# Sparse attention with the softmax weights as the stationary matmul operand, values with a ones column moving, and masks added by bf16 products

## Chip, cores and metric

One core of a Trainium2 chip. The metric is device microseconds of one execution. The kernel before takes 2502.95 us (median of 3 runs, 2499.74 to 2503.1).

## What is computed

One layer of a decoder trunk: 1024 tokens, width 1024. The part that changes is the sparse attention (NSA): 16 heads in 4 groups of 4, head size 64, three branches per head.

```python
s_c = einsum(q, kc) - slopes * dist_c                       # 63 compressed keys
p_c = softmax(where(dist_c >= 0, s_c, NEG)) * any_valid     # also chooses the key blocks
o_cmp = einsum(p_c, vc)
o_slc = selection_branch(q, rmsnorm(k_s), v_s, top_k blocks)  # softmax over chosen 64-token blocks
o_win = window_branch(q, rmsnorm(k_w), v_w)                 # softmax over the last 256 tokens
o = gates[..., 0:1] * o_cmp + gates[..., 1:2] * o_slc + gates[..., 2:3] * o_win
```

Around it stand the input projections with a gated DeltaNet (before), and the output projections and the MLP (after).

## The kernel before

The program is one recorded list: each step is a Python function that is put at a time and a rank by `at` (L312), and all are called in that order (L1373). Each engine gets its instructions in an order fixed at build time and runs them in that order.

**Stages.** Projections and DeltaNet come first, then the sparse attention, then output projection and MLP. The sparse attention has 32 items (L1358): group g of 4, query tile t of 8 (128 queries, 4 heads each). An item (L1105) has these steps, put by `at3` (L1098) at times around its number i, so that steps of several items interleave, together with the DeltaNet output projection (`dn_part`, tiles `g`):

- `cmp_scores` (L1131) to `cmp_out` (L1199): the compressed branch. A product with three rows of position terms (`far`, `onesr`, L1134) and two with the keys make scores in a PSUM tile `m` of a ring of two. VectorE adds the mask and takes the minimum head by head (L1142), ScalarE takes the exponential, VectorE multiplies by gate and inverse sum (L1171), TensorE transposes (L1184) and multiplies by the values (L1196); the result `acc` stands as channels by queries.
- `peak` (L1204): scores of each head against all keys (tiles `S`), whose minimum VectorE takes (L1217).
- `weights` (L1236), once for each key tile of 128 and branch (0 selection, 1 window), 228 times in all: two products into a PSUM tile `T` (128 keys by 4 heads x 128 queries), at the edge of the mask two more with a triangular `cap` (L1246: bf16, 64x64 blocks, tiles `cb`; 88 key tiles have them), then ScalarE writes the exponentials `P`. GpSimd adds the `P` tiles of a branch into `sum` (L1253, L1256).
- `values` (L1260): for each key tile two products, one for each pair of heads, with the values `vv` as the stationary operand (128 keys x 64 channels) and half of `P` moving (256 columns). The results go to two 64-row halves of PSUM tile `O`, which has a region of its own for each branch.
- `total` (L1266), `share` (L1271), `join` (L1281), once for each branch: two products with a matrix of ones sum `sum` over keys, VectorE transposes, inverts, multiplies by a gate (`gq`) and transposes back, then multiplies `O` by it, GpSimd adds to `acc`, and after branch 1 a DMA stores it to `ond`.

`gq` is a copy of the gates in a transposed layout, made once in `gating` (L407 to L417) by four products and 16 copies. `sparse_setup` (L1026) loads the constants.

All operands of `values`, `total` and of the products with the compressed keys and values are plain f32; TensorE runs such a product as two instructions. Each of these has a weight load (LDWEIGHTS) of its own.

Of the kernel before, what the change touches and what calls it, by code (L numbers as in the profile page):

```python
# [35 lines left out]
         ("msel", "mwin", "mcmp", "okm", "addm", "hot", "capd", "capw", "edge"))  # L36
# [6 lines left out]
def constants():  # L43
# [20 lines left out]
    c64 = np.arange(64)[None, :]  # L64
    capd = np.where(p % 64 <= c64, 0, 1e30).astype(f)
    capw = np.where(p % 64 > c64, 0, 1e30).astype(f)
# [26 lines left out]
    for br in range(2):  # L93
        for hl in range(2):
# [5 lines left out]
                 mwin=mwin, mcmp=mcmp, hot=hot, capd=capd, capw=capw, edge=edge, anyv=anyv, okm=okm, addm=addm)  # L100
# [48 lines left out]
def body(ctx: ExitStack, tc: tile.TileContext, A, out):  # L149
# [50 lines left out]
    def load_consts(pool, i):  # L200
        n = f"cst{i}"
        w = A[n].shape[1]
        cst[i] = pool.tile([128, (w + 63) // 64 * 64 if i == 2 else w], F32, name=n, bufs=1)[:, 0:w]
        SY.dma_start(cst[i], A[n])
# [182 lines left out]
    gq = PL.cq.tile([128, 2, NT, NG, 8], F32, name="gq")  # L387
# [8 lines left out]
    def gating():  # L396
# [9 lines left out]

        for qb in range(4):  # L407
            sl = pb.tile([128, 4, 32], F32, name="sl", bufs=2)
            V.tensor_copy(sl, ident[:, 32 * qb:32 * qb + 32].unsqueeze(1).to_broadcast([128, 4, 32]))
            pg = PL.ps.tile([128, NT, 4, 4, 3], F32, name="s")  # L410
            mm(pg.rearrange("p t g r c -> p (t g r c)"), sl.rearrange("p a b -> p (a b)"),
               gates.rearrange("p t c -> p (t c)"), True, True)
            for hf in range(2):
                for br in range(2):
                    o = slice(64 * hf, 64 * hf + 64)
                    V.tensor_copy(gq[o, br, :, :, qb::4].rearrange("p t g a -> p (t g) a"),
                                  pg[o, :, :, 2 * hf:2 * hf + 2, br + 1].rearrange("p t g a -> p (t g) a"))  # L417
# [605 lines left out]

    msel = mwin = mcmp = okm = addm = hot = ones = identb = capd = capw = onesr = far = QC = nsp = mts = O = None

    def sparse_setup():  # L1026
        nonlocal msel, mwin, mcmp, okm, addm, hot, ones, identb, capd, capw, onesr, far, QC, nsp, mts, O
# [3 lines left out]
        mcmp = K("mcmp").rearrange("p (t c) -> p t c", t=8)  # L1031
# [3 lines left out]
        ones = K("ones")  # L1035

        onesr = pn.tile([128, 128], F32R, name="onesr")
        identb, capd, capw = [pn.tile([128, w], BF16, name=f"cb{i}") for i, w in enumerate((128, 64, 64))]
        for o, n in ((identb, "ident"), (capd, "capd"), (capw, "capw"), (onesr, "ones")):
            V.tensor_copy(o, K(n))  # L1040
# [42 lines left out]
    def values_of(g):  # L1083
        for br in range(2):
            SY.dma_start(kk[g][2][:, :, br, :],
                         nvd[br, :, 64 * g:64 * g + 64].rearrange("(t p) c -> p t c", p=128))
# [16 lines left out]
    kk = {}  # L1103

    def item(i, g, t):  # L1105
# [25 lines left out]
        def cmp_scores():  # L1131
            psc = PL.pm.tile([128, 4, 64], F32, name="m")
            o = slice(32 * g, 32 * g + 3)
            mm(g2(psc), onesr[o], far[o], True, False)  # L1134
# [4 lines left out]
            sm = PL.pn.tile([128, 4], F32, name="csm", bufs=2)  # L1139
            for r in range(4):  # L1140
                o = 2 * (r % 2) + r // 2
                V.tensor_tensor_reduce(pc[:, o, :], psc[:, r, :], mcmp[:, t, :], 1.0, 3e38,  # L1142
                                       OP.add, OP.min, mx[:, o:o + 1])
            for r in range(4):
                act(pc[:, r, :], pc[:, r, :], AF.Exp, scale=-1.0, bias=mx[:, r:r + 1], accum_out=sm[:, r:r + 1])
            X["pc"], X["sm"] = pc, sm

        def cmp_choose():
            pc, sm = X["pc"], X["sm"]
            rc = PL.pn.tile([128, 4], F32, name="rc", bufs=2)  # L1150
# [20 lines left out]
            V.tensor_tensor(pc, pc, rc.unsqueeze(2).to_broadcast([128, 4, 64]), OP.mult)  # L1171

        def choice():
            X["ch"] = p = PL.pm.tile([80, 128], F32, name="m")
# [6 lines left out]
        def cmp_turn():  # L1181
            p = PL.pm.tile([128, 2, 128], F32, name="m")
# [9 lines left out]
        def cmp_values():  # L1192
            pT = X["pT"]
            p = PL.pm.tile([128, 256], F32, name="m")
            for b in range(2):
                mm(p[:, b * 128:(b + 1) * 128], vcb[:, g, :], pT[:, b, :], True, True)  # L1196
            X["acc"] = p

        def cmp_out():  # L1199
            p = X["acc"]  # L1200
            X["acc"] = acc = PL.pn.tile([128, 256], F32, name="acc", bufs=4)
            act(acc, p)
# [24 lines left out]
        def peak_rows():  # L1227
            X["pk"] = p = PL.pm.tile([112, 128], F32, name="m")
# [7 lines left out]
        def weights(br, k):  # L1236
# [7 lines left out]
            if cap is not None:  # L1244
                for q in Q2:
                    mm(ps[q, :, q], identb[q, q], cap[q].unsqueeze(1).to_broadcast([64, 4, 64]), False, True)  # L1246
            P = PL.pr.tile([128, 4, 128], F32, name="P", bufs=5)
            act(P, ps, AF.Exp, scale=-1.0)
            X[br, k] = P
            if spans[br][1] == 1:  # L1250
                X["sum", br] = P
            elif ("sum", br) in X:
                adds.tensor_tensor(X["sum", br], X["sum", br], P, OP.add)  # L1253
            elif ("one", br) in X:
                X["sum", br] = s = PL.pr.tile([128, 4, 128], F32, name=f"sum{br}", bufs=2 - br)
                adds.tensor_tensor(s, X.pop(("one", br)), P, OP.add)  # L1256
            else:
                X["one", br] = P

        def values(br, k, first, last):  # L1260
            vv = kk[g][2]
            P = X.pop((br, k))
            for hf in range(2):
                mm(O[hf * 64:hf * 64 + 64, br], vv[:, k, br, :], g2(P[:, 2 * hf:2 * hf + 2, :]), first, last)

        def total(br):  # L1266
            X["tot", br] = p = PL.pm.tile([128, 2, 128], F32, name="m")
            for hf in range(2):
                mm(p[hf * 64:hf * 64 + 64], ones[:, 0:64], g2(X["sum", br][:, 2 * hf:2 * hf + 2, :]), True, True)

        def share(br):  # L1271

            b = PL.pr.tile([128, 256], F32, name="bs", bufs=3)
            V.transpose(b, g2(X["tot", br]))
            c = PL.pr.tile([128, 16], F32, name="coef", bufs=4)[:, 0:8]
            V.reciprocal(c, b[:, 0::32])
            V.tensor_tensor(c, c, gq[:, br, t, g], OP.mult)
            X["bs", br] = b = PL.pr.tile([128, 256], F32, name="bs", bufs=3)
            V.transpose(b, c.unsqueeze(2).to_broadcast([128, 8, 32]))

        def join(br):  # L1281
            b = X["bs", br]
            V.tensor_tensor(b, O[:, br], b, OP.mult)  # L1283
            acc = X["acc"]
            GP.tensor_tensor(acc, acc, b, OP.add)
            if br == 1:
                SY.dma_start(ond[2 * g:2 * g + 2, :, t * 128:(t + 1) * 128].rearrange("a p q -> p a q"),
                             acc.rearrange("p (a q) -> p a q", a=2))
# [464 lines left out]
```

## Time and profile before

| what | value |
|---|---|
| median of 3 runs | 2502.95 us |
| the profiled execution | 2501.7 us, span 2499.9 us |
| TensorE (PE) busy | 2423.2 us, 97% of the span, 14193 matmul instructions |
| VectorE (DVE) / ScalarE (ACT) / GpSimd (POOL) busy | 1680.0 / 1099.2 / 768.4 us |
| sparse stage, about 1104 to 1668 us | PE, DVE, ACT, POOL work together |

A busy PE is not a PE at its peak: the modelled end of a matmul lies after the start of the next. So for PE the distance from one start to the next is read, which is what an instruction costs the queue. "Idle before" is time in which an engine did nothing, and the name behind the arrow is what ended it.

### The profile page before, as it was taken

The numbers are of one execution on the slowest core, as the hardware profiler recorded it, in microseconds if no ns is written. First come the engines' busy times: TensorE is split into PE (matmuls) and PEld (weight loads), VectorE is DVE, ScalarE is ACT, GpSimd is POOL, SyncE is SP. The second block draws the span as 40 slices with busy tenths as digits, with TensorE's granted clock in tenths as the row PEclk, the third lists the DMA queues.
The fourth block names the chain that finished last, engine by engine and source line by source line (L and its number), as shares of the span: only waits on it lengthen the run. The fifth ranks groups of instructions, "written<-read, shape, count | busy, mean of one in ns | idle before, by whom it ended". The sixth has DMA issues, their size and how long they took to land. (4 is left out here: it accounts for less than half of the span.)

```text
span 2499.9 us, 40066 instructions
## 1 busy us (share of the span) xinstructions
PE 2423.2 (97%) x14193; PEld 1865.5 (75%) x14193; DVE 1680.0 (67%) x4006; ACT 1099.2 (44%) x2258; POOL 768.4 (31%) x622
## 2 busy tenths in 40 slices
PE   8999999999999999999999999999998999989999
PEld 5787878788887888765555555558877888868887
DVE  7666574837576665368788797964368666586685
ACT  4233343434443442346565655442236555534443
POOL 3132220303132321003534445432135443360230
PEclk9999999999999999999999999999999999999999
DMA  5421313122221312264232322126433444477343
GB/s 174 126 76 45 86 44 88 48 79 63 62 66 57 82 48 82 73 174 129 87 85 73 110 60 72 47 80 217 162 124 131 144 156 144 149 256 231 120 125 102
DMA packets 237353, 267.17 MB, mean 107 GB/s; under 512 B 76961, under 2 KB 128481, under 8 KB 237025
## 3 DMA queue, kind: packets, MB, share of 16 engines
q1 hardware_dynamic: 237152, 264.61, 34.3%
q8 instruction: 112, 1.84, 0.3%
q14 instruction: 89, 0.72, 0.1%
HBM read 190.12 MB, written 72.38 MB: 105 GB/s over the span
## 5 line engine op out<-in xcount | busy, mean ns | idle before, releaser
L179 PE MATMUL g<-hh,wh 128*128 128x512 f32 (+1 forms) x816 | 336.0, 412 | 6.5 <-ACT hh L176 6.1
L179 PE MATMUL g<-hl,wh 128*128 128x512 f32 (+1 forms) x816 | 328.7, 403 | 0.1
L179 PE MATMUL g<-hh,wl 128*128 128x512 f32 (+1 forms) x816 | 323.9, 397 | 0.0
L179 PE MATMUL V<-big,wh 128*128 128x512 f32 x768 | 239.0, 392 | 2.4 <-DVE c L1596 2.4
L188 DVE TENSOR_TENSOR wl<-a,wh 128x512 fp32r<-128x512 f32 x192 | 160.3, 836 | 112.2 <-ACT wh L176 111.9
L176 ACT ACTIVATE wh<-wr 128x512 fp32r<-128x512 f32 x210 | 132.0, 629 | 216.1 <-PE g L179 137.7
L176 ACT ACTIVATE wh<-a 128x512 fp32r<-128x512 f32 x192 | 121.0, 630 | 222.0 <-PE V L179 112.3
L1217 DVE CUSTOM_DVE_ANT_0 junk<-S,cst 128x384 f32<-128x384 f32 (+3 forms) x320 | 167.7, 528 | 63.1 <-PE S L179 61.9
L279 DVE TENSOR_TENSOR wl<-wr,wh 128x512 fp32r<-128x512 f32 x178 | 127.5, 720 | 113.4 <-ACT wh L176 110.2
L176 ACT ACTIVATE P<-T 128x512 f32<-128x512 f32 x228 | 134.2, 594 | 144.8 <-PE T L179 124.7
L179 PEld LDWEIGHTS g<-hh,wh 128*128 128x128 f32 (+1 forms) x816 | 153.8, 188 | 35.2 <-ACT hh L176 6.1
L179 PEld LDWEIGHTS g<-hh,wl 128*128 128x128 f32 (+1 forms) x816 | 153.6, 188 | 29.7 <-issue 0.6
L179 PEld LDWEIGHTS g<-hl,wh 128*128 128x128 f32 (+1 forms) x816 | 154.0, 189 | 26.6 <-DVE hl L326 1.3
L179 PEld LDWEIGHTS V<-big,wh 128*128 128x128 f32 x768 | 144.6, 189 | 33.5 <-ACT c L176 2.0
L1253 POOL TENSOR_TENSOR sum<-sum,P 128x512 f32<-128x512 f32 x101 | 133.7, 1324 | 70.1 <-ACT P L176 67.7
L179 PE MATMUL V<-big,wl 128*128 128x512 f32 x384 | 150.3, 391 | 3.2 <-DVE wl L188 3.2
L179 PE MATMUL g<-wh,hh 128*128 128x256 f32 x512 | 147.5, 288 | 0.0
L179 PE MATMUL o<-P,vv 128*64 128x256 f32 x912 | 144.2, 399 | 1.8 <-DVE bs L1283 1.6
L179 PE MATMUL g<-wl,hh 128*128 128x256 f32 x512 | 144.8, 283 | 0.0
L179 PE MATMUL g<-wh,hl 128*128 128x256 f32 x512 | 144.8, 283 | 0.0
L179 PE MATMUL S<-ks,qc 96*128 96x384 f32 (+3 forms) x320 | 122.9, 397 | 6.8 <-DVE mx L1217 6.3
L1453 POOL TENSOR_TENSOR a<-a,a 128x512 f32<-128x512 f32 x32 | 51.1, 1596 | 254.5 <-DVE wl L188 228.5
(378 smaller groups left out, 6010.0 us busy)
## 6 DMA issues: line engine op xcount, KB each, us to landing
bb<-acd SPq DMA_DIRECT2D x112, 256.0 KB, 2.8
wr<-in_w_dn_dram SPq DMA_DIRECT2D x64, 256.0 KB, 2.7
a<-in_w_u_dram SPq DMA_DIRECT2D x64, 256.0 KB, 3.3
acd<-c SPq DMA_DIRECT2D x64, 256.0 KB, 2.3
a<-in_w_d_dram SPq DMA_DIRECT2D x64, 256.0 KB, 5.0
wr<-in_w_nb_dram SPq DMA_DIRECT2D x32, 256.0 KB, 2.6
wr<-in_w_gt_dram SPq DMA_DIRECT2D x32, 256.0 KB, 2.6
gtd<-fx SPq DMA_DIRECT2D x32, 256.0 KB, 2.1
```

The source lines that it names most:

```text
L176: return SC.activation(o, i, fn, **kw)
L179: return PE.matmul(o, l, r, start=start, stop=stop, skip_group_check=True)
L188: V.tensor_tensor(lo, src, f(hi), OP.subtract)
L279: V.tensor_tensor(wl, wr, f(wh), OP.subtract)
L1217: V.tensor_tensor_reduce(junk[:, :w], ps[:, :w], mask[:, a:b], 1.0, 3e38, OP.add, OP.min, o)
L1253: adds.tensor_tensor(X["sum", br], X["sum", br], P, OP.add)
L1453: (eng or GP).tensor_tensor(o, a, b, OP.subtract)
```

## The change

`values` swaps its operands: `P` (64 queries of one head) is stationary, and the values move, with a column of ones as 65th; eight products for a key tile. `O` then stands as queries by channels, and its column 64 is the softmax sum. So `total`, `share`, the `sum` additions and `gq` go. `O` is now one region for both branches. The values of two key tiles follow each other. `join` divides by column 64; after branch 1 `turn_out` transposes `acc` back on TensorE and `turn_store` copies and stores it. The triangular caps become one bf16 product of 512 columns; the mask of the compressed scores is added by a bf16 product too, and the position terms use all 128 rows with a selecting column `gsel`. VectorE takes the four minima of the compressed scores in one reduction, and multiplies by gate and inverse sum where the branch's result is read (`cmp_out`).

```diff
-        for qb in range(4):
...
-            mm(pg.rearrange("p t g r c -> p (t g r c)"), sl.rearrange("p a b -> p (a b)"),
-               gates.rearrange("p t c -> p (t c)"), True, True)
...
+        for o, sign, base in ((capd, 1, 0), (capw, -1, -1)):
+            GP.memset(o, 0.0)
+            GP.affine_select(o, o, [[sign, 128]], OP.is_ge, 1e30, base=base, channel_multiplier=-sign)
+        maskb = pn.tile([128, 8, 64], BF16, name="maskb")
...
-        O = PL.po.tile([128, 2, 256], F32, name="o")
+        O = PL.po.tile([128, 4, 128], F32, name="o")
...
-        vv = p.tile([128, NT, 2, 64], F32, name="vv")
+        vv = p.tile([128, NT, 2, 128], F32, name="vv")
+        GP.memset(vv[:, :, :, 64:65], 1.0)
...
-            mm(g2(psc), onesr[o], far[o], True, False)
+            mm(g2(psc), gsel[:, g:g + 1].to_broadcast([128, 128]), far, True, False)
+            mm(psc, identb, maskb[:, t:t + 1, :].to_broadcast([128, 4, 64]), False, False)
...
+            V.tensor_reduce(mx, psc, axis=AX.X, op=OP.min)
             for r in range(4):
                 o = 2 * (r % 2) + r // 2
-                V.tensor_tensor_reduce(pc[:, o, :], psc[:, r, :], mcmp[:, t, :], 1.0, 3e38,
-                                       OP.add, OP.min, mx[:, o:o + 1])
-            for r in range(4):
-                act(pc[:, r, :], pc[:, r, :], AF.Exp, scale=-1.0, bias=mx[:, r:r + 1], accum_out=sm[:, r:r + 1])
+                act(pc[:, o, :], psc[:, r, :], AF.Exp, scale=-1.0, bias=mx[:, r:r + 1], accum_out=sm[:, o:o + 1])
...
-            V.tensor_tensor(pc, pc, rc.unsqueeze(2).to_broadcast([128, 4, 64]), OP.mult)
+            X["rc"] = rc
...
-                mm(p[:, b * 128:(b + 1) * 128], vcb[:, g, :], pT[:, b, :], True, True)
+                mm(p[:, b * 128:(b + 1) * 128], pT[:, b, :], vcb[:, g, :], True, True)
...
-            act(acc, p)
+            V.tensor_tensor(acc, p, X["rc"].unsqueeze(2).to_broadcast([128, 4, 64]), OP.mult)
...
-                for q in Q2:
-                    mm(ps[q, :, q], identb[q, q], cap[q].unsqueeze(1).to_broadcast([64, 4, 64]), False, True)
-            P = PL.pr.tile([128, 4, 128], F32, name="P", bufs=5)
+                mm(ps, identb, cap.unsqueeze(1).to_broadcast([128, 4, 128]), False, True)
+            P = PL.pr.tile([128, 4, 128], F32, name="P", bufs=6)
...
-            if spans[br][1] == 1:
-                X["sum", br] = P
-            elif ("sum", br) in X:
-                adds.tensor_tensor(X["sum", br], X["sum", br], P, OP.add)
...
-            for hf in range(2):
-                mm(O[hf * 64:hf * 64 + 64, br], vv[:, k, br, :], g2(P[:, 2 * hf:2 * hf + 2, :]), first, last)
-        def total(br):
...
-        def share(br):
...
+            for r in range(4):
+                for q in Q2:
+                    mm(O[q, 2 * (r % 2) + r // 2, 0:65], P[:, r, q], vv[:, k, br, 0:65], first and r == 0, last)
         def join(br):
-            b = X["bs", br]
-            V.tensor_tensor(b, O[:, br], b, OP.mult)
+            c = PL.pr.tile([128, 64], F32, name="coef", bufs=2)[:, 0:4]
+            V.reciprocal(c, O[:, :, 64])
+            V.tensor_tensor(c.rearrange("p (b a) -> p b a", b=2), c.rearrange("p (b a) -> p b a", b=2),
+                            gt.rearrange("p (a b) c -> p b a c", a=2)[:, :, :, br + 1], OP.mult)
+            b = PL.pr.tile([128, 4, 64], F32, name="bs", bufs=2)
+            V.tensor_tensor(b, O[:, :, 0:64], c.unsqueeze(2).to_broadcast([128, 4, 64]), OP.mult)
             acc = X["acc"]
-            GP.tensor_tensor(acc, acc, b, OP.add)
...
+            adds.tensor_tensor(acc, acc, b, OP.add)
+        def turn_out():
+            X["out"] = p = mtile(128, 2, 128)
+            for b in range(2):
+                PE.transpose(p[:, b, :], g2(X["acc"][:, 2 * b:2 * b + 2, :]), ident)
+        def turn_store():
+            o = PL.pr.tile([128, 2, 128], F32, name="ot", bufs=2)
+            act(o, X["out"])
+            SY.dma_start(ond[2 * g:2 * g + 2, :, t * 128:(t + 1) * 128].rearrange("a p q -> p a q"), o)
...
+            j0 = j - (0 if br == 0 else t + 1)
+            e = i + (j + (j0 % 2 == 0 and not last)) / n + lag
+            times.append(e)
+            at3(e, values, br, k, first, last)
```

The order of the instructions moves with it. TensorE around the end of the window branch (branch 1) of group 1, query tile 6, before. `o` is `O`, `cst_114` with `sum` the matrix of ones, `T`/`S`/`m` are the PSUM tiles named above; a program row with x2 is two products:

```order
L179 MATMUL o<-P,vv 64x256 x2
L179 MATMUL S<-ks,qc_11341 128x128
L179 MATMUL T<-qd,kd 128x512
L179 MATMUL T<-qc_11348,ks 128x512
L179 MATMUL m<-sum_14752,cst_114 64x256 x2
L179 MATMUL o<-P,vv 64x256 x2
L179 MATMUL m<-far,onesr 128x256
L179 MATMUL m<-kcb,qn 128x128 x2
L179 MATMUL T<-qd,kd 128x512
L179 MATMUL T<-qc_11348,ks 128x512
L179 MATMUL S<-ks,qc_11341 128x128
L179 MATMUL o<-P,vv 64x256 x2
```

The first row is the branch's last key tile; the next item's first key tile follows five rows below and its second at the end. The same place after the change:

```order
L177 MATMUL o<-vv,P 64x65 x8
L177 MATMUL S<-ks,qc_11318 128x128
L177 MATMUL T<-qd,kd 128x512
L177 MATMUL T<-qc_11325,ks 128x512
L177 MATMUL m<-far,gsel 128x256
L177 LDWEIGHTS cb_11296
L177 MATMUL m<-maskb,cb_11296 128x256
L177 MATMUL m<-kcb,qn 128x128 x2
L177 MATMUL T<-qd,kd 128x512
L177 MATMUL T<-qc_11325,ks 128x512
L177 MATMUL S<-ks,qc_11318 128x128
L177 MATMUL o<-vv,P 64x65 x16
```

The total has gone, the next item's first two key tiles are one run of 16 products at the end, and a mask product stands behind `far`.

VectorE at the same place before (`share`, then the compressed scores of a later item; ISA rows of L1142 are its minima):

```order
L1274 STREAM_TRANSPOSE bs<-m 128x256
L1276 RECIPROCAL coef<-bs 128x8
L1277 TENSOR_TENSOR coef<-coef,gq 128x8
L1279 STREAM_TRANSPOSE bs<-coef 128x256
L1142 ISA pc,cmx<-m,cst_11327 128x64
```

`join` (L1283) follows behind the other minima. After the change (`join` in the rows of `coef` and `bs`; rows of L1223 are `peak`'s minima, `cmx` is the reduction of the compressed scores):

```order
L1208 TENSOR_TENSOR acc<-m,rc 128x256
L1266 RECIPROCAL coef<-o 128x4
L1223 ISA junk,mx<-S,cst_11294 128x128
L1267 TENSOR_TENSOR coef<-coef,gates 128x4
L1270 TENSOR_TENSOR bs<-o,coef 128x256
L1148 TENSOR_REDUCE cmx<-m 128x4
```

Between the first and the last reading of `O` (L1266, L1270) stands work of another item.

## Rows read from the trace of the kernel before

**Rows 1.** The page's busy time of TensorE (busy us, share of the span, instructions) and its granted clock in 40 slices, and the sparse stage without its start, from the view of stretches (length, then busy us of each engine with its instructions, granted clock, DMA share, GB/s).

```profile
PE 2423.2 (97%) x14193; PEld 1865.5 (75%) x14193; DVE 1680.0 (67%) x4006; ACT 1099.2 (44%) x2258; POOL 768.4 (31%) x622
PEclk9999999999999999999999999999999999999999
...
1121.00:1668.00 547.00, 532.99 (x2790) 304.50 (x2790) 449.12 (x1613) 304.51 (x754) 250.22 (x218) 1.00 0.27 79
```

**Rows 2.** The timeline of TensorE at several places in the sparse stage: start us, length us, engine, line, operation, tiles, shape, instructions merged in the row, idle time before with its releaser. The distance between two starts is what the earlier row cost.

```profile
1438.82 0.38 PE L1184 MATMUL m<-cst,pc 128*128 128x128 f32 x2
1438.95 0.47 PE L179 MATMUL T<-qc,ks 128*128 128x512 f32 x1
...
1566.21 0.39 PE L179 MATMUL T<-qd,kd 128*128 128x512 f32 x1
1566.53 0.38 PE L179 MATMUL m<-far,onesr 3*128 3x256 f32 x1
1566.83 0.71 PE L179 MATMUL m<-kcb,qn 128*128 128x128 f32 x4
...
1568.31 1.08 PE L179 MATMUL o<-P,vv 128*64 128x256 f32 x8
1569.33 0.31 PE L1175 MATMUL m<-cst,nsp 128*80 128x128 f32 x1
...
1660.27 0.40 PE L179 MATMUL T<-qc,ks 128*128 128x512 f32 x1
1660.60 0.30 PE L179 MATMUL T<-cb,cb 64*64 64x256 bf16 x2
1660.82 0.65 PE L179 MATMUL o<-P,vv 128*64 128x256 f32 x4
1661.41 0.50 PE L179 MATMUL T<-qd,kd 128*128 128x512 f32 x1
...
1665.65 0.65 PE L179 MATMUL m<-sum,cst 128*64 128x256 f32 x4
1666.23 0.50 PE L179 MATMUL g<-oh,wl 128*128 128x512 f32 x1
...
1669.43 0.39 PE L179 MATMUL g<-oh,wh 128*128 128x512 f32 x1
1669.66 0.39 PE L179 MATMUL g<-ol,wh 128*128 128x512 f32 x1
```

**Rows 3.** The timeline of TensorE in the DeltaNet stage, where eight products of 128x64 stationary and 64 moving columns, in turn to the two 64-row halves, stand in a row (`kT`); columns as in group 2. The product before it is of the 128*128 form, the one behind it of the 128*64 form.

```profile
346.90 0.38 PE L179 MATMUL c<-St,wq 128*128 128x128 f32 x2
347.21 0.69 PE L179 MATMUL s<-kT 128*64 128x64 f32 x16
347.72 0.58 PE L179 MATMUL tp<-cst,tmp 128*64 128x1 f32 x16
```

**Rows 4.** Groups of TensorE instructions by line and form (instructions, then busy us, mean ns of one, idle us before with its releasers): the gate products of `gating`, and the weight loads (PEld) of the `kT` products.

```profile
L179 PE MATMUL s<-gates,sl 128*128 128x384 f32 x8 | 3.0, 502 | 0.4 <-DVE gates L405 0.4
L179 PEld LDWEIGHTS s<-kT 128*64 128x64 f32 x256 | 10.1, 137 | 2.0 <-issue 0.4
```

**Rows 5.** Groups of VectorE and GpSimd instructions by line and form, 1104 to 1668 us, columns as in group 4, and one row of the view of tile `coef` in the same stretch (ns min/median/max, first and last start).

```profile
L1274 DVE STREAM_TRANSPOSE bs<-m 128x256 f32<-128x256 f32 x64 | 28.3, 442 | 14.6 <-PE m L179 11.6 <-POOL sum L1256 2.6
L1279 DVE STREAM_TRANSPOSE bs<-coef 128x256 f32<-128x256 f32 x64 | 28.1, 439 | 0.5
L1283 DVE TENSOR_TENSOR bs<-o,bs 128x256 f32<-128x256 f32 x63 | 26.2, 416 | 1.2 <-PE o L179 0.4
L1277 DVE TENSOR_TENSOR coef<-coef,gq 128x8 f32<-128x8 f32 x64 | 21.3, 333 | 0.6
L1142 DVE CUSTOM_DVE_ANT_0 pc<-m,cst 128x64 f32<-128x64 f32 x120 | 20.3, 213 | 10.4 <-PE m L179 10.1
L1171 DVE TENSOR_TENSOR pc<-pc,rc 128x256 f32<-128x256 f32 x31 | 18.3, 589 | 0.1
L1142 DVE DVE_READ_ACCUMULATOR2_ANT cmx<- 128x1 f32 x120 | 9.8, 82 | 0.0
...
L1253 POOL TENSOR_TENSOR sum<-sum,P 128x512 f32<-128x512 f32 x101 | 133.7, 1324 | 70.1 <-ACT P L176 67.7
L1256 POOL TENSOR_TENSOR sum<-P 128x512 f32<-128x512 f32 x54 | 70.5, 1305 | 150.9 <-ACT P L176 150.8
...
L1277 DVE TENSOR_TENSOR coef<-coef,gq x64: 152/166/1256, 1122.1 to 1667.3; 128x8 f32<-128x8 f32 x64
```

**Rows 6.** The timeline of TensorE, VectorE and GpSimd at two branch ends: the total, and VectorE's answer to it (L1274); columns as in group 2.

```profile
1437.35 0.65 PE L179 MATMUL m<-sum,cst 128*64 128x256 f32 x4
1440.11 0.43 DVE L1274 STREAM_TRANSPOSE bs<-m 128x256 f32<-128x256 f32 x1
...
1523.01 0.65 PE L179 MATMUL m<-sum,cst 128*64 128x256 f32 x4
1523.78 0.45 DVE L1274 STREAM_TRANSPOSE bs<-m 128x256 f32<-128x256 f32 x1 [0.88 <-POOL sum L1256]
1523.92 1.28 POOL L1253 TENSOR_TENSOR sum<-sum,P 128x512 f32<-128x512 f32 x1
1524.27 0.20 DVE L1276 RECIPROCAL coef<-bs 128x8 f32<-128x8 f32 x1
1524.51 0.71 DVE L1277 TENSOR_TENSOR coef<-coef,gq 128x8 f32<-128x8 f32 x1
```

**Rows 7.** Who waited for whom, 1104 to 1668 us: us in total, times, the longest.

```profile
PEld S L179 <- DVE mx L1217: 18.9, 35, 1.5
PEld o L179 <- DVE bs L1283: 7.4, 16, 1.1
```

More of the change, by code (lines that the diff above doesn't have):

```diff
@@ L63, in constants @@
     mcmp = np.where((pos >= cc * 16 + 31) & (cc < NCMP), 0, BIG).astype(f).reshape(128, 512)
-    c64 = np.arange(64)[None, :]
-    capd = np.where(p % 64 <= c64, 0, 1e30).astype(f)
-    capw = np.where(p % 64 > c64, 0, 1e30).astype(f)
+    gsel = ((p // 32 == np.arange(4)[None, :]) & (p % 32 < 3)).astype(f)
     th = np.arange(16)[None, :]
@@ L1034, in sparse_setup @@
         hot = K("hot").rearrange("p (r q) -> p r q", r=4)
[L1035 to L1040, printed above, removed]
+        identb, capd, capw = [pn.tile([128, 128], BF16, name=f"cb{i}") for i in range(3)]
+        V.tensor_copy(identb, K("ident"))
+        for o, sign, base in ((capd, 1, 0), (capw, -1, -1)):
+            GP.memset(o, 0.0)
+            GP.affine_select(o, o, [[sign, 128]], OP.is_ge, 1e30, base=base, channel_multiplier=-sign)
+        maskb = pn.tile([128, 8, 64], BF16, name="maskb")
+        raw = pn.tile([128, 512], F32, name="junk", bufs=2)
+        SY.dma_start(raw, A["cst2"][:, AT["mcmp"][1]:])
+        V.tensor_copy(flat(maskb), raw)
+        gsel = pn.tile([128, 64], F32R, name="gsel")[:, 0:NG]
+        V.tensor_copy(gsel, K("gsel"))
         raw = pn.tile([128, 256], F32, name="junk", bufs=2)
@@ L1103, in body, with mtile, finish_items @@
     kk = {}
+    def mtile(*shape):
+        return PL.pm.tile(list(shape), F32, name="m")
+    times, ends = [], []
+    def finish_items():
+        for e, join, turn_out, turn_store, br in ends:
+            e = min([x for x in times if x >= e], default=e) + 1e-6
+            at3(e + 0.08, join, br)
+            if br:
+                at3(e + 0.3, turn_out)
+                at3(e + 0.4, turn_store)
     def item(i, g, t):
@@ L1149, in cmp_choose @@
             pc, sm = X["pc"], X["sm"]
-            rc = PL.pn.tile([128, 4], F32, name="rc", bufs=2)
+            rc = PL.pn.tile([128, 4], F32, name="rc", bufs=4)
             V.reciprocal(rc, sm)
@@ L1181, in cmp_turn @@
         def cmp_turn():
-            p = PL.pm.tile([128, 2, 128], F32, name="m")
+            p = mtile(128, 2, 128)
             for b in range(2):
@@ L1227, in peak_rows @@
         def peak_rows():
-            X["pk"] = p = PL.pm.tile([112, 128], F32, name="m")
+            X["pk"] = p = mtile(112, 128)
             PE.transpose(p, f(mts[i % 2]), ident)
@@ L1321, in item @@
             last = j == n - 1 or tiles[j + 1][0] != br
-            at3(i + j / n + lag, values, br, k, first, last)
+            j0 = j - (0 if br == 0 else t + 1)
+            e = i + (j + (j0 % 2 == 0 and not last)) / n + lag
+            times.append(e)
+            at3(e, values, br, k, first, last)
             if last:
-                e = i + j / n + lag
-                at3(e + 0.07, total, br)
-                at3(e + 0.15, share, br)
-                at3(e + 0.25, join, br)
+                ends.append((e, join, turn_out, turn_store, br))
     D_ = {}
@@ L1371, in body @@
         item(i, g, t)
+    finish_items()
     for e in sorted(due, key=lambda e: e[:3]):
```

53 lines of the change are left out of this document (12 added, 41 removed).

## The prediction

> **What bounds the kernel now.** I read the page first, then the view of stretches for the stage that changes, then TensorE's timeline there. TensorE is busy for 97% of the span at the full clock, and in the sparse stage for 533 of 547 us; VectorE has 449, ScalarE 305, GpSimd 250 [rows 1]. So the stage lasts as long as TensorE's queue, and a change is worth what it takes from the distances between starts. "Busy" can't show this, because a product's modelled end lies behind the next start.
>
> The timeline gives these distances [rows 2]. A full 512-column product costs 0.23 us (1669.43 to 1669.66). A group of `values` for two key tiles costs 1.02 us (1568.31 to 1569.33), for one 0.59 (1660.82 to 1661.41): so each further tile costs 0.43, and 0.16 is paid once in each group, for the first weight load and for going back to full 128-column products. Going in costs too: the product ahead of a 64-wide one takes 0.33 instead of 0.23 (1660.27 to 1660.60), so 0.10. **One visit to the 64-wide form thus costs 0.26 us** beside its work. The caps (64x64) pay 0.10 and then 0.22 (1660.60 to 1660.82); `far`, with three rows, pays 0.09 and then 0.30 (1566.21, 1566.53, 1566.83).
>
> **The change on TensorE.** Counts are from the program; visits are counted in the two orders of the instructions.
>
> Before:
> - `values`: 228 key tiles x 0.43 = 98.0 us.
> - `total`: 64 x 0.43 = 27.5 (a group alone costs 0.58, like `values` [rows 2]).
> - 223 visits to the 128x64 form (values and totals that adjoin count once) x 0.26 = 58.0; 44 of them are next to a cap or `far` without a full product between, so one way is saved: -4.4.
> - 88 caps x 0.32 = 28.2; 32 `far` x 0.39 = 12.5.
> - Sum: 219.8 us.
>
> After:
> - `values` as eight products for a tile. The trace has this very form in the DeltaNet stage: `kT`, 128x64 stationary, 64 columns moving, in turn to the two 64-row halves. Sixteen instructions (eight products) cost 0.51 us from start to start [rows 3], of which I take 0.05 for the first load (the 0.16 above without 0.10 for going back, which is taken to cost what going in does). So 0.46, and with 65 columns 0.47, for each tile: 228 x 0.47 = 107.2 us. Bounds: 0.43, as now, and 0.59, a group's whole price now.
> - 153 visits x 0.26 = 39.8. The pairing makes most of this: the order above shows a run of 16.
> - 88 caps as full products x 0.23 = 20.2, without a visit.
> - `gsel` and mask products, 256 columns: half of 0.23 each, 64 x 0.12 = 7.7. Bounds 0.11 and 0.23, so up to 7 us more.
> - `turn_out`: 64 transposes. Two cost 0.13, and the next product is longer by 0.08 (1438.82, 1438.95 [rows 2]): 64 x 0.11 = 7.0.
> - Sum: 181.9 us.
>
> **Net 219.8 - 181.9 = 38 us less.** In `gating` eight instructions of 3.0 us go from an early stage in which TensorE is the bound too [rows 4]: 3 us less.
>
> **The change elsewhere.** VectorE loses both transposes (28.3 + 28.1) and the four minima of the compressed scores with their reads (20.3 + 9.8), and gains 32 reductions of 256 elements; nearest row, the 256-element read of PSUM in `join`, 0.42: 13. The gate multiply (18.3) becomes a read of PSUM of 0.42 x 32 = 13. The coefficient product stays, its 8 elements now 4. GpSimd loses 155 additions, 204 us [rows 5]. Those hold VectorE up: L1277, with 8 elements and two inputs, takes 0.15 at least and 1.26 at most, 0.33 on the mean against a median of 0.17 [rows 5], and where it took 0.71 a GpSimd addition ran beside it until 1525.20 [rows 6]. So VectorE falls from 449 to some 370 us or less. This is cover, not a gain, while TensorE is the bound; only where TensorE waits for VectorE it is one: weight loads of `S` waited 18.9 us for `peak`'s minima, those of `O` 7.4 for `join` [rows 7]. I take 8 us less; bounds 0 and 26.
>
> ScalarE loses `cmp_out` (32) and gains `turn_store` (32) of the same size: nothing. `P` waits for two tiles instead of one, with six buffers for five. In `sparse_setup` a mask load and its cast come ahead of the first `far`: 1 us at most, left out.
>
> **The added wait.** `O` has one region where it had two. The next branch's first product must wait until `join` has read it, and behind it on TensorE's in-order queue stands everything. There are 63 such places. What covers the wait is the work between the last and the next `values`: adding the prices above along the new order gives 1.1 to 7.0 us, the middle one 2.7, 1.8 at the place that the order shows. What must fit is VectorE's answer plus `join`. The answer was 0.12 us at one branch end (1523.66 to 1523.78) and 2.1 at another (1438.00 to 1440.11) [rows 6]. `join` is 0.20 + 0.17 + 0.42 = 0.8 us [rows 5, 6], and with other items' work that stands between in the new order up to 1.7 mostly. With the quick answer 1.9 fits into 2.7; with the slow one 3.8 doesn't, and 1.1 is lost. VectorE has less to do, so I am nearer to the quick one: 1 place in 7 slow, 63 x 0.16 = 10 us. Bounds 0 and 63 x 1.1 = 69.
>
> **Sum**: -38 - 3 - 8 + 10 = -39 us. The profiled execution took 2501.7 us (span 2499.9), 1.2 under the median of 2502.95. 2501.7 - 39 = 2462.7; I say **2464**.
>
> **A rule against it.** Each product of `values` now has its own weights: 16 loads for a tile instead of 4. In the trace a load of this form lasts 137 ns [rows 4], yet 16 instructions with their loads take 0.51 us [rows 3], so the loads are hidden behind each other and the products. The Trainium skill, "TensorE: Matmul & The Clock Gate", section "LDWEIGHTS (loading the stationary operand)", gives a load as its columns divided by 1.2, in ns: 53 for 64 columns, thus 0.85 us for a tile's 16 if nothing overlapped, and an estimate of 2464 + 228 x 0.38 = 2551. The trace does not agree with such a sum for this form.
>
> **Rivals.**
> 1. *Weight loads become the bound* (slower). If the two halves load side by side but each pair of products waits for its pair of loads, a tile costs 8 x 137 ns = 1.10 us instead of 0.47: 228 x 0.63 = 144 more, 2608. For it: `P` is fresh from ScalarE, unlike `kT`. Against it: rows 3. Chance 0.03. It is the skill's rule above in this kernel's durations.
> 2. *The single `O` stalls TensorE* (slower). The saving without that wait, 49 us, is 0.78 us for each of 63 branch ends; from there on the kernel is slower. At the slow answer everywhere (1.1 us): 2501.7 - 49 + 69 = 2522. For it: that answer is in the trace, and `join` is split by other work. Against it: the quick answers, and VectorE's falling load. Chance 0.06.
> 3. *Half of it is lost*: TensorE's starts wait on others more than rows 7 tell, or `O` costs half its bound (35 us). 2501.7 - 49 + 35 = 2488, or half the net saving, 2482. Chance 0.21.
> 4. *The waits vanish too*: no wait at `O`, all 26 us of rows 7 gone: 2501.7 - 41 - 26 = 2435. TensorE's remaining queue allows it; that every such wait goes is unlikely. Chance 0.05 for under 2445.
> 5. *The pairs don't come together on the chip*, so that visits stay as many as now: 70 more visits cost 18 us, 2482. The order is fixed at build time and shows the runs; this lies within case 3.
>
> **How the numbers follow.** The forecast, 2464 with 2448 to 2478 as its own range (the mask products 7 up, rows 7 and `O` by some 10 either way, the price of a tile 0.02 either way, 5 us), has 0.65. The range of 2446 to 2496 takes in nearly all of case 3; it leaves out rival 1, most of rival 2 and case 4. A difference of 0.2%, 5 us, is about what a measurement can tell from none. Faster: forecast, case 4 and nearly all of case 3, 0.88. Within 0.2%: 0.05, the near end of rivals 2 and 3. Slower: 0.07.
>
> **What would show it.** Right: `o` in 1824 products (3648 instructions) with pairs of starts some 58 ns apart, 16 instructions in about half a microsecond; 153 visits; `m<-sum` and the 155 GpSimd additions gone; L1277's successor under 0.2 us; the stage from 1104 to 1668 shorter by some 36 us, and all that follows as before. Wrong: idle time ahead of `o` with `coef` or `bs` as its releaser above 20 us (rival 2); `kT`-like groups above 0.6 us (rival 1); the same number of products in a stage that hardly shrank (case 3).

## The result, and the profile after

The changed kernel takes **2423.03 us** (median of 4 runs, 2422.39 to 2424.2) against 2503.02 (4 runs beside them): ratio 0.9681, 95% interval 0.9664 to 0.9697. That is 80 us less, where 39 were forecast, and below the stated range of 2446 to 2496. Its profiled execution took 2423.24 us.

Nearly all of it lies in the sparse stage. From the first `T` product to the last `o` product it lasted 1104.3 to 1667.4 us before, 563.1 us, and lasts 1103.1 to 1588.9 now, 485.8 us: 77 less. What follows took 832.5 us and takes 832.6.

The page's row of busy time and the row of this stretch (columns as in [rows 1]), after:

```profile
PE 2355.4 (97%) x16673; PEld 1921.2 (79%) x16673; DVE 1565.8 (65%) x3626; ACT 1092.0 (45%) x2258; POOL 565.7 (23%) x473
...
1103.10:1588.90 485.80, 482.15 (x5323) 369.21 (x5323) 347.82 (x1324) 307.35 (x785) 48.61 (x65) 0.99 0.33 94
```

The same stretch of the kernel before, for the comparison of like with like:

```profile
1104.30:1667.40 563.10, 547.10 (x2843) 313.18 (x2843) 459.05 (x1670) 314.48 (x785) 250.15 (x218) 0.99 0.28 80
```

TensorE is still busy nearly throughout, with almost twice the instructions; VectorE fell by 111 us, GpSimd by 202. ScalarE fell by 7, and the granted clock stayed at 0.99.

TensorE's timeline after (columns as in [rows 2]), two visits to the 128x64 form; it answers to the `o` rows of [rows 2] and to [rows 3]:

```profile
1575.47 0.40 PE L177 MATMUL T<-qc,ks 128*128 128x512 f32 x1
1575.80 0.69 PE L177 MATMUL o<-vv,P 128*64 128x65 f32 x16
1576.41 0.50 PE L177 MATMUL T<-qd,kd 128*128 128x512 f32 x1
1576.75 0.39 PE L177 MATMUL T<-qc,ks 128*128 128x512 f32 x1
1576.98 0.40 PE L177 MATMUL T<-qd,kd 128*128 128x512 f32 x1
1577.21 0.40 PE L177 MATMUL T<-qc,ks 128*128 128x512 f32 x1
1577.45 0.39 PE L177 MATMUL g<-oh,wh 128*128 128x512 f32 x1
1577.76 1.15 PE L177 MATMUL o<-vv,P 128*64 128x65 f32 x32
1578.85 0.50 PE L177 MATMUL T<-qd,kd 128*128 128x512 f32 x1
1579.18 0.39 PE L177 MATMUL T<-qc,ks 128*128 128x512 f32 x1
```

Read the starts. One tile takes 0.61 us (1575.80 to 1576.41), two take 1.09: 0.47 to 0.48 for each further tile. The product ahead of a visit takes 0.33 (1575.47 to 1575.80) and 0.31 (1577.45 to 1577.76) instead of 0.23 (1576.75 to 1576.98). And the product **behind** it takes 0.34 (1576.41 to 1576.75), 0.33 at 1578.85: a third charge, which the forecast does not have. A visit thus costs 0.34 to 0.35 us beside its work, where the forecast had 0.26. Over all such places of the stage the median of a 512-column product is 0.337 us behind a visit (42 places) against 0.232 between full products (539); before it was the same 0.337 (83 places). The rows had shown it: 1661.41 in [rows 2] is a `T` product of 0.50 us behind a visit, where others are 0.39 long (its modelled length; the start behind it is not among those rows).

The tile `coef` after (columns as in its row of [rows 5]):

```profile
L1266 DVE RECIPROCAL coef<-o x63: 160/181/183, 1117.5 to 1586.3; 128x4 f32<-128x4 f32 x63
L1267 DVE TENSOR_TENSOR coef<-coef,gates x63: 145/158/166, 1118.0 to 1586.5; 128x4 f32<-128x4 f32 x63
L1270 DVE TENSOR_TENSOR bs<-o,coef x63: 403/419/427, 1118.7 to 1586.8; 128x256 f32<-128x256 f32 x63
```

The coefficient product, which took up to 1256 ns before, never takes over 166 now. And the waits of TensorE for VectorE's minima and for `join` in the stage, columns as in [rows 7]:

```profile
PEld S L177 <- DVE mx L1223: 5.6, 17, 0.9
PEld o L177 <- DVE bs L1270: 2.1, 6, 0.4
PEld o L177 <- DVE mx L1223: 1.9, 6, 0.4
PE S L177 <- DVE mx L1223: 1.2, 4, 0.7
```

18.9 and 7.4 us [rows 7] have become 5.6 and 2.1.

**An account of the stage.** I priced every start-to-start distance of TensorE in both traces with what the same instruction costs undisturbed (512 columns 0.229 us, 384 0.177, and so on; a tile of `values` 0.43 before, 0.467 after) and with the charges of a form change as above. What is left over is called the rest: waits, and what the prices miss.

| sparse stage, us | before | after | difference |
|---|---|---|---|
| products | 414.1 | 415.2 | +1.1 |
| form changes (303 returns to full products, then 153) | 106.1 | 52.3 | -53.8 |
| rest | 42.9 | 18.3 | -24.6 |
| stage | 563.1 | 485.8 | -77.3 |

So the products themselves cost the same. The forecast had 38 less for products and form changes together, where it is 53, and 2 more for waits, where it is 25 less. The split between the two last rows hangs on the prices: with prices fitted to all the traces at once (a product's own, what stands ahead of it and what behind) the rest falls by 14 to 19 us instead of 25, and form changes by as much more. The experiments test both.

### The profile page after: what moved, and what is told of

It reads as the page before. It is cut to its first block, busy times and chain, and to the rows that moved or that the text cites. A ratio compares the mean times of both kernels' runs of the same rounds, so it can differ in the third digit from the quotient of the medians.

```text
span 2421.5 us, 44385 instructions
## 1 busy us (share of the span) xinstructions
PE 2355.4 (97%) x16673; PEld 1921.2 (79%) x16673; DVE 1565.8 (65%) x3626; ACT 1092.0 (45%) x2258; POOL 565.7 (23%) x473
## 5 line engine op out<-in xcount | busy, mean ns | idle before, releaser
L1223 DVE CUSTOM_DVE_ANT_0 junk<-S,cst 128x384 f32<-128x384 f32 (+3 forms) x320 | 168.4, 532 | 66.2 <-PE S L177 62.7
L177 PEld LDWEIGHTS o<-vv,P 128*64 128x64 f32 x3648 | 120.3, 137 | 39.7 <-issue 27.9
L1272 POOL TENSOR_TENSOR acc<-acc,bs 128x256 f32<-128x256 f32 x62 | 48.2, 778 | 414.8 <-DVE bs L1270 292.9
L177 PE MATMUL o<-vv,P 128*64 128x65 f32 x3648 | 141.5, 226 | 0.0
```

Source lines behind the costliest of these rows:

```text
L177: return PE.matmul(o, l, r, start=start, stop=stop, skip_group_check=True)
L1223: V.tensor_tensor_reduce(junk[:, :w], ps[:, :w], mask[:, a:b], 1.0, 3e38, OP.add, OP.min, o)
L1272: adds.tensor_tensor(acc, acc, b, OP.add)
```

## Experiments

Each kernel ran beside the kernel before, whose median was 2500.6 to 2503.3 us in the four groups of runs; a ratio is to that median. Stage and busy times are from the view of stretches, from the first `T` product of `weights` to the last `o`, and are those of one execution of each kernel. Differences of 2 us between them say nothing: the stage of a_acc_v is 2.1 us shorter than that of the changed kernel, its median 2.0 longer. Visits are groups of 128x64 products of `values` and `total`; "rest" is that of the account above.

| kernel | median us | ratio (95% interval) | stage | visits | VectorE busy | GpSimd busy | rest |
|---|---|---|---|---|---|---|---|
| before | 2503.02 | 1 | 563.1 | 223 | 459.1 | 250.2 | 42.9 |
| after | 2423.03 | 0.9681 (0.9664-0.9697) | 485.8 | 153 | 347.8 | 48.6 | 18.3 |
| a_single | 2440.28 | 0.9759 (0.9745-0.9774) | 503.5 | 218 | 348.8 | 48.4 | 13.7 |
| a_four | 2411.31 | 0.9642 (0.9627-0.9656) | 472.4 | 102 | 345.9 | 49.2 | 22.4 |
| a_cap64 | 2433.38 | 0.973 (0.9715-0.9744) | 494.3 | 147 | 348.5 | 48.8 | 16.2 |
| a_full | 2463.74 | 0.9853 (0.9837-0.987) | 529.9 | 0 | 345.7 | 49.1 | |
| b_cap128 | 2494.26 | 0.9964 (0.9952-0.9977) | 554.9 | 230 | 453.9 | 251.7 | 44.1 |
| a_sums | 2447.86 | 0.9775 (0.9757-0.9794) | 511.5 | 153 | 408.3 | 254.2 | 43.7 |
| a_turns | 2427.52 | 0.9699 (0.9682-0.9715) | 489.5 | 156 | 388.8 | 48.6 | 21.0 |
| a_both | 2457.47 | 0.9816 (0.9793-0.9838) | 521.9 | 156 | 450.5 | 252.5 | 53.1 |
| b_nosum | 2491.37 | 0.9962 (0.9946-0.9977) | 550.7 | 229 | 392.4 | 47.3 | 28.6 |
| a_acc_v | 2425.02 | 0.969 (0.9665-0.9716) | 483.7 | 150 | 358.2 | 0.4 | 17.2 |
| a_sums_v | 2450.92 | 0.979 (0.9765-0.9815) | 513.3 | 150 | 435.5 | 203.9 | 46.6 |
| a_copy_v | 2425.42 | 0.9695 (0.9663-0.9726) | 484.2 | 150 | 375.2 | 107.5 | 17.7 |

### Form changes: a_single, a_four, a_cap64, b_cap128

```diff
-            e = i + (j + (j0 % 2 == 0 and not last)) / n + lag
+            e = i + j / n + lag                                       # a_single
+            e = i + (j - j0 + min(j0 - j0 % 4 + 3, end)) / n + lag    # a_four; end: the branch's last; P with 9 buffers
```

> The changed kernel with the values of each key tile on their own instead of two tiles at a time (and join 0.02 earlier in its time, so that it stays ahead of the next branch). Visits to the 128x64 form rise from 153 to 218, by 65; the products stay the same. Theory A (a visit costs 0.34 us, since the full product behind it is slowed by 0.10 us too, which my forecast left out): 65 x 0.34 = 22 us more, 2445. Rival P (0.26 us for a visit, as forecast; what else was gained are waits on other engines): 65 x 0.26 = 17 us more, 2440. Rival W (form changes are cheap, the pairs gave TensorE slack): under 10 us more. In the trace, a full product behind a visit is longer by 0.10 us from start to start for A, by nothing for P.

> The changed kernel with the values of up to four key tiles together, with 9 buffers for P in place of 6 (room made by vv 65 wide, one buffer for coef and one for ot). Visits fall from 153 to 102, by 51. Theory A: 51 x 0.34 = 17 us less, 2406, if the longer distance from the weights to their use brings no new wait. Rival P: 51 x 0.26 = 13 us less, 2410. Between this kernel and the one with single tiles lie 116 visits: A says 40 us, P says 30. Rival W: no gain, or a loss, since P waits longer and its buffers run out (ScalarE waits for o).

65 more visits made the stage 17.7 us longer, 51 fewer made it 13.4 shorter: 0.27 and 0.26 us a visit; the medians of these two kernels lie 29 us apart, 0.25 for each of 116 visits. That is the forecast's price in time, though the distances show 0.34. The rest moves the other way (13.7, 18.3, 22.4), which fits that a part of what a visit costs TensorE lies in time that it would else have waited; the rest is a remainder of single executions, so this is not shown. Theory A holds for the distances, and rival P for the time of these kernels: the saving was not paid out in full.

```diff
-                mm(ps, identb, cap.unsqueeze(1).to_broadcast([128, 4, 128]), False, True)
+                for q in Q2:                                           # a_cap64; b_cap128 is the reverse in the kernel before
+                    mm(ps[q, :, q], identb[q, q], cap[q, q].unsqueeze(1).to_broadcast([64, 4, 64]), False, True)
```

> The changed kernel with the triangular caps as two 64x64 products again, 256 columns each, as in the kernel before. That adds some 89 visits to the 64x64 form, 62 of them apart from the visits of the values. Theory A: the two products take 0.11 us of streaming where the one of 512 columns takes 0.23, but an own visit costs 0.10 ahead, 0.115 at its end and 0.10 on the product behind: +0.19 each for 68, nothing for 21 that adjoin a visit of the values: 13 us more, 2436. Rival P (the product behind is not slowed: +0.09): 6 us more, 2429.

> The kernel before with each triangular cap as one product of 128x128 stationary and 512 moving columns, as in the changed kernel. The 92 visits to the 64x64 form go; TensorE leaves another form for a full product 247 times instead of 303. Theory A: 10 us more of streaming (92 x 0.115) and some 22 less of form changes, 12 less: 2489. Rival P (a cap costs 0.32 in a form of its own against 0.23): 92 x 0.09 less the places that adjoin another visit, some 6 less: 2495.

The stage was 8.5 us longer with the small caps, and 8.2 shorter without them in the kernel before: between A and P both times, and what the forecast had for the caps (28.2 to 20.2, 8 us). The visits of `values` moved with the order, 6 fewer and 7 more, so the caps alone were worth one or two us more than that.

### Full stationary operands: a_full

```diff
-                for q in Q2:
-                    mm(O[q, 2 * (r % 2) + r // 2, 0:65], P[:, r, q], vv[:, k, br, 0:65], first and r == 0, last)
+                mm(O[:, 2 * (r % 2) + r // 2, 0:65], P[:, r, :], vv[:, k, br, 0:65], first and r == 0, last)
```

> The changed kernel with full stationary operands in values: P of all 128 queries of a head (128x128), four products for a key tile instead of eight, the same 65 moving columns, O written over 128 rows at once. No form changes are left in the sparse stage. Theory A with loads: the visits go, 153 x 0.34 = 52 us less; but each instruction is then bound by its load of 128 columns, 109 ns as in the products with vcb, 8 instructions 0.87 us for a tile against 0.467 for the sixteen whose two halves run side by side: 228 x 0.40 = 92 more. Net +40, 2463. If loads hide as they do for the halves (58 ns for an instruction): 52 less, 2371.

2463.7, as the first theory said: 0.43 us more for each of 228 tiles and 153 visits less at 0.34 make 45 us, and the stage was 44.1 longer. So where the loads set TensorE's pace, a visit was paid at its full price. TensorE's timeline of it:

```profile
1304.97 0.39 PE L177 MATMUL T<-cb,cb 128*128 128x512 bf16 x1
1305.20 1.90 PE L177 MATMUL o<-vv,P 128*128 128x65 f32 x16
1306.90 0.48 PE L177 MATMUL S<-ks,qc 96*128 96x512 f32 x1
1307.22 0.27 PE L1235 MATMUL m<-cst,mts 128*112 128x128 f32 x1
```

Two tiles take 1.70 us (1305.20 to 1306.90) against 1.09 in halves. Nothing is charged ahead (0.23). The product behind takes 0.32, where 0.23 is usual, but this is no charge: the `o` products ahead of it start 0.112 us apart, and 16 x 0.112 + 0.232 = 2.02, which is what group and product behind take together (1305.20 to 1307.22). The start between them has only moved.

### The loads of VectorE and GpSimd: a_sums, a_turns, a_both, b_nosum

```diff
+            elif ("sum", br) in X:                        # a_sums: as in the kernel before, in weights
+                adds.tensor_tensor(X["sum", br], X["sum", br], P, OP.add)
...
+            y = PL.pr.tile([128, 256], F32, name="tz", bufs=1)   # a_turns: in join
+            V.transpose(y, msel[:, 0:256])
+            V.transpose(y, msel[:, 0:256])
...
+            X["sum", br] = P                              # b_nosum: kernel before, all additions gone
```

> The changed kernel with GpSimd's additions of the P tiles put back (155 of 128x512, 1.3 us each), their result read by no one (vv is 65 wide to make room; one buffer for each branch's sum). TensorE's own work is that of the changed kernel. What TensorE's starts cost beyond products and form changes in the sparse stage, taken from the distances between starts, fell from 43 us before to 18 after. Theory G (GpSimd's additions hold VectorE up, and VectorE holds TensorE up): most of these 25 us come back, 15 to 25 more, 2438 to 2448. Rival V (VectorE's own work did it): under 5 more, 2423 to 2428. Rival T (it was the total with its answer, and the ring of m tiles): nothing, 2423.

> The changed kernel with two VectorE transposes of 128x256 more in each join (of constant data, read by no one; vv 65 wide): 128 x 0.44 = 56 us of VectorE's time, as in share before. Rival V: 56 of the some 110 us that VectorE lost come back, so some half of the 25 us of waits, and since they stand ahead of the reading of the single O, more: 2435 to 2445. Theory G: VectorE has slack once GpSimd leaves it alone; up to 5 more for O alone: 2423 to 2428. Rival T: 2423.

> The changed kernel with both of these: GpSimd's 155 additions and VectorE's 128 transposes. If the two add up, the sum of the two differences; if they act through each other (transposes lengthened or late by the additions), more than the sum. If all of the 25 us lie in VectorE's delay: 2448 or more. Rival T: 2423.

> The kernel before without GpSimd's additions: the total is taken of the last key tile's P alone, and share adds 1 to it in place of the inverse, so this part of the computation is left out. TensorE's products are those of the kernel before. Theory G: 15 to 25 less, 2478 to 2488. Rival V: under 5 less, 2498 to 2503; the same for rival T.

The additions bring the stage back by 25.7 us, the transposes by 3.7, both together by 36.1: more than the sum, though the medians (24.8, 4.5 and 34.4) say so by 5 us only, about their noise. **a_both is the pivot.** It has about the VectorE and GpSimd time of the kernel before (450.5 and 252.5 us against 459.1 and 250.2), and TensorE's work of the changed one; its stage of 521.9 us lies 41 under the one before and 36 above the one after. Who waited for whom in its stage:

```profile
PEld S L177 <- DVE mx L1223: 20.3, 36, 1.3
PEld o L177 <- DVE bs L1282: 18.5, 24, 2.0
PE o L177 <- DVE bs L1282: 10.7, 14, 1.7
PE S L177 <- DVE mx L1223: 10.0, 18, 1.1
```

The first and the last row are the kernel before again; the two between are the single `O`, 29 us in two overlapping views, where the changed kernel has 2.1. So the added wait is dear when VectorE answers late and nearly free when it doesn't.

b_nosum met neither theory: 9.2 us less than before, 12.4 in the stage, where G had 15 to 25 and its rivals under 5. Its coefficient product, without the additions, never took more than 169 ns:

```profile
L1269 DVE TENSOR_TENSOR coef<-coef,gq x63: 146/163/169, 1124.2 to 1656.1; 128x8 f32<-128x8 f32 x63
```

So the same additions are worth some 12 us of stage in the kernel before and 26 to 32 in the changed one (a_sums against after, a_both against a_turns). The single `O` is one reason that fits, TensorE's shorter queue another; no run separates them.

### What in the additions holds it up: a_acc_v, a_sums_v, a_copy_v

```diff
-            adds.tensor_tensor(acc, acc, b, OP.add)
+            V.tensor_tensor(acc, acc, b, OP.add)                         # all three, in join
...
+                adds.tensor_tensor(X["sum", br], X["sum", br], P, OP.add)  # a_sums_v
+                GP.tensor_copy(X["sum", br], P)                          # a_copy_v instead
```

> The changed kernel with the additions to acc on VectorE instead of GpSimd, which then has nearly nothing left in the sparse stage; the base for the next two. VectorE gains some 62 additions of 128x256 (0.3 to 0.6 us each), loses what GpSimd's additions hold it up. 2420 to 2428.

> The same with GpSimd's 155 additions of P tiles put back, read by no one: no instruction on any engine needs a result of GpSimd here. Theory H (GpSimd's additions hold VectorE's two-input instructions up, and TensorE waits for VectorE): 10 to 16 us more than with acc on VectorE alone, as the kernel before gains without its additions; VectorE's coefficient product has a mean of twice its median. Rival Q (with the additions put back and acc on GpSimd, the loss of 24 us was the queue on GpSimd, behind which acc and with it turn_out stood): under 5 us more.

> The same as the last, with GpSimd copying P (one input) instead of adding it (two inputs), at the same 155 places. If only two-input instructions of GpSimd hold VectorE up: the time of the kernel with acc on VectorE alone, within 4 us, and a coefficient product of VectorE at its median throughout. If any GpSimd instruction that reads and writes the same memory does: in proportion to GpSimd's busy time, up to what the additions cost.

In a_sums `turn_out` had also waited for GpSimd's queue (12.3 us of weight loads for `acc`). Here nothing does, and the additions still cost 29.6 us of stage (25.9 in the medians). TensorE waits for the minima more than for `join`:

```profile
PEld S L177 <- DVE mx L1223: 27.9, 49, 2.5
PE S L177 <- DVE mx L1223: 14.2, 26, 2.0
PEld o L177 <- DVE bs L1279: 8.1, 14, 1.4
```

The coefficient product and GpSimd's work with additions:

```profile
L1276 DVE TENSOR_TENSOR coef<-coef,gates x62: 147/159/1252, 1121.0 to 1608.3; 128x4 f32<-128x4 f32 x62
...
L1258 POOL TENSOR_TENSOR sum<-sum,P 128x512 f32<-128x512 f32 x101 | 132.6, 1313 | 69.7 <-ACT P L174 66.8
L1261 POOL TENSOR_TENSOR sum<-P 128x512 f32<-128x512 f32 x54 | 71.0, 1314 | 214.9 <-ACT P L174 214.9
```

and with copies:

```profile
L1276 DVE TENSOR_TENSOR coef<-coef,gates x64: 146/158/568, 1117.6 to 1589.6; 128x4 f32<-128x4 f32 x64
...
L1258 POOL COPY sum<-P 128x512 f32<-128x512 f32 x108 | 70.5, 653 | 128.0 <-ACT P L174 127.1
L1261 POOL COPY sum<-P 128x512 f32<-128x512 f32 x56 | 36.6, 654 | 236.1 <-ACT P L174 236.1
```

A short VectorE product is held for as long as GpSimd's instruction at most: 1.25 us beside additions of 1.31, 0.57 beside copies of 0.65. The starts and ends show who holds it: each coefficient product of over 0.3 us (22 before, 18 with additions, 10 with copies) ends 11 to 26 ns behind the end of a GpSimd addition or copy that ran beside it, and none without such a neighbour took over 0.17. So copies hold it up too, which the first reading of that expectation excluded; but the stage is 0.5 us longer than without them. TensorE rode out the copies' holds and not the additions'. Whether the length of a hold or their sum counts is not separated, since both are halved. Theory H stands, its cost above its 10 to 16 us, and Q falls.

### What was left: b_none, a_twoO, a_four_v

```diff
-            V.transpose(b, g2(X["tot", br]))              # b_none: b_nosum without share's transposes
...
+        O = [PL.po.tile([128, 4, 128], F32, name=f"o{i}") for i in range(2)]   # a_twoO; ("m", 2) is ("m", 1)
```

a_four_v is a_four with `acc` added on VectorE, as above.

> The kernel before without GpSimd's additions and without VectorE's two transposes for each branch: the total is taken of the last key tile alone, its answer (an addition and the coefficient product on 8 columns) goes nowhere, and join multiplies O by ones; that part of the computation is left out. TensorE's products are those of the kernel before, VectorE and GpSimd have about the load that they have in the changed kernel. Theory L (the loads of both engines, acting together, were worth 36 us of the sparse stage, which is what returned when both were put back in the changed kernel): 30 to 36 us less than before, 2465 to 2472. Rival S (they only matter together with the changed kernel's order, in which TensorE has less to do; in the old one the additions' 10 are all): 2487 to 2493.

> The changed kernel with a region of O for each branch, in two banks (the two m tiles share one bank for that). The build then puts some other products between those of a visit, so that there are 169 visits in place of 153: 16 x 0.27 to 0.34 = 4 to 5 us more. If the single O costs my 10 us: 2418. If it costs 2, as the waits after the change say: 2425 to 2427.

> Values of four key tiles together and the additions to acc on VectorE. By the two differences alone (12 less than the changed kernel, and 0 to 2 from the stage with acc on VectorE): 2408 to 2412.

b_none: 2497.5 us, ratio 0.9981 (0.9968-0.9995), stage 560.9. That is above the ranges of L and S both. The build set the products into another order, with 257 visits instead of 229; its rest is 30.8, b_nosum's 28.6. Stage and rest are those of its slowest execution of ten, 2504.87 us. At 0.27 us each, the 28 more visits would make 7.6, an estimate that brings the median into the range of S. So theory L is not borne out, and the run doesn't show what the transposes alone were worth. a_twoO: 2437.87 us, 0.973 (0.9705-0.9754), stage 496.4, which is 10.6 longer, of which 16 more visits explain 4 to 5; the `m` tiles in one bank may be the rest. It is outside both of its forecasts and says nothing on the price of `O`. a_four_v: 2410.83 us, 0.9624 (0.9603-0.9645); with a_four it is the fastest here, some 12 us below the changed kernel.

## Why the prediction was wrong, step by step

- **TensorE as the bound of the stage**: right. Every gain is one in its starts.
- **`values` as eight products, 0.47 us a tile, 153 visits**: right. The groups of `o` take 131.5 us from start to start in all; 228 x 0.47 + 153 x 0.16 is 131.6. The single pairs came 58 ns apart.
- **A visit at 0.26 us**: mis-sized in the distances, which show 0.34. The 0.10 on the product behind was missed, at visits, caps and `far` alike; so products and form changes fell by 53 us or more and not by 38. In time the visits of a_single and a_four paid 0.25 to 0.27 and the caps 8 us, as forecast, and those of a_full about 0.34; so how much of the 80 us this step explains can't be said to better than these 15.
- **"This is cover, not a gain": VectorE's and GpSimd's relief at 8 us, bounds 0 and 26**: this is the step that failed. VectorE fell to 348 us, within the forecast; but putting the loads back into the changed kernel costs 36 us (a_both) and the additions alone 26 to 30. In the kernel before, taking the additions out gave 9 to 12, near the forecast's 8. So the step failed in what the change made of the old loads: the forecast set a price on their relief in the old queue and added it to TensorE's saving and the wait for `O`, as if the three did not touch. Two readings helped to mislead. Rows 7 are two rows of a view whose rows for TensorE and its weight loads behind VectorE, which overlap, sum to 67 us before and 16 after. And the 8 us has no working of its own between its bounds. Nor does VectorE's busy share tell the price: a_turns, with VectorE at 389 of 489.5, pays 3.7 us and a_sums, at 408 of 511.5, pays 25.7. What sets these two apart is the longest hold, the 1256 in [rows 5]; but taking that hold away gave b_nosum only its 9 to 12.
- **The single `O` at +10 us**: too much, since it hung on the same step. The waits for `join` sum to 2.1 us; with the old loads (a_both) they come to some 29 in two overlapping views.
- **`gating`, 3 us**: the stage begins 1.2 us earlier; it begins between 1100.2 and 1107.2 in kernels that are alike up to there, so this can't be told.
- **The rivals**: none was right. The nearest is the fourth, that the waits vanish; its bound of 26 us was rows 7 again.

The sum: forecast -36 in the stage (38 less, 8 less, 10 more); measured -41 with the old loads and another -36 from their relief. Taken the other way round, the additions gave 12 and all else the other 65. Both are right; the parts don't add up as the forecast had them.

What stays open: of the 24.6 us of rest that went, GpSimd's additions are worth 14.3 in the kernel before (42.9 to 28.6). The other ten were not located, and b_none did not find them in the transposes. They may be prices rather than waits: with the fitted prices the rest falls by 14 to 19, and the additions' part of it in the kernel before is 14 again. Why the old loads cost the changed kernel so much more than the old one is argued and not shown.

## What to carry to other kernels

Where an engine ahead of the bound answers late now and then, look at the longest time of its short instructions beside their median, and ask who holds them. Taking a two-input elementwise stream off GpSimd was worth 26 to 30 us in the changed kernel and 9 to 12 in the old one, so price such a relief in the queue that the change leaves. Price a change of TensorE's form by three distances, the product ahead, the group and the product behind, and only by their sum, since a start can move from one to the next; and expect some of a saving on TensorE to turn into waits. A wait that a change adds is worth what the answering engine's worst case makes it, so cost it after the relief that the same change brings, not before.

## What the runs showed of the hardware

- **Loads of two halves run side by side.** Full loads of 128 columns gave 8 instructions in 0.81 us and 16 in 1.70 (a_full), so 0.112 us for each more; in 64-column halves a pair starts every 58 ns, the two 6 ns apart (after). The moving columns are 65 in both, so the pace follows the load's columns. The forecast said that the loads were hidden behind each other and the products; they seem to set the pace. The Trainium skill, "TensorE: Matmul & The Clock Gate", section "LDWEIGHTS (loading the stationary operand)", gives a load as its columns divided by 1.2, so 107 and 53 ns. The traces agree with it within 5 ns for one load at a time (112) and for one pair of halves (58), and not for the sum over all sixteen that the forecast weighed.
- **A slow product behind a group need not be a charge.** Behind the `o` products of a_full a 512-column product takes 0.315 us, and 0.316 behind transposes before, against 0.232. But the starts ahead are early by as much: 0.027 from the last transpose to the product behind it, where a transpose takes 0.11. In both cases group and product behind sum to what they cost apart. Behind a visit to the 128x64 form they do not, and the 0.337 there is paid.
- **A GpSimd copy holds VectorE's two-input instructions up too**, but for half as long (0.57 us at most against 1.25), and at no price in a_copy_v (0.5 us of stage).
